# Grouped-query attention in a one-core backbone step: row maxima of two heads on the two halves of the contraction rows, and key tiles taken in twos

## The chip, the cores and the metric

The program runs on one core of one Trainium2 chip. The metric is the device time of one execution in microseconds (us); lower is better. Three executions of the kernel before gave 3754.33, 3758.16 and 3764.13 us (median 3758.16). A profile of a further execution was taken; that execution took 3772.03 us and its trace spans 3770.2 us.

## What is computed

The reference is one layer of a hybrid diffusion backbone on 256 context tokens and 2048 latent tokens: modulation, one joint input projection, three mixers in parallel (differential attention, grouped-query attention, a bidirectional state-space scan), an output projection with normalisation, and a SwiGLU feed-forward part. The change is in the grouped-query attention of the latent tokens (with one small part in the loading of the output projection's weights):

```
scale = 64 ** -0.5
qg = q.reshape(b, t, 2, 2, 64)           # 2 key/value heads, each with 2 query heads
s  = einsum('bqkgd,bskd->bkgqs', qg, k) * scale
p  = softmax(s, axis=-1)
o  = einsum('bkgqs,bskd->bqkgd', p, v)
```

There are 2048 queries and 2560 keys (2048 latent, 512 cached). Before the exponential, a bound near the row's maximum is subtracted.

## The kernel before

**Work and order.** `attention` (from L841) does the differential heads first, then the grouped heads. The order of instructions of TensorE, VectorE (DVE), ScalarE (ACT) and GpSimd (POOL) is the order in which the Python code emits them; generators are advanced by hand, each `yield` being a place where other work is put in. Each engine runs its own stream in order and waits on semaphores.

**Units.** The grouped heads are cut into 8 units (`units`, L934): a key/value head j and a block of 512 queries. A unit serves the two query heads r = 0, 1 of j. Queries and keys are held as two numbers each (a high part in F32R and a rest). `qa` is a tile [128, 2, 512] with the high parts in rows 0 to 63 and the rests in rows 64 to 127; `qb` has the high parts in rows 0 to 63 and, in row 64, the negated maxima. `gk[j][:, 0]` holds the keys' high parts twice (rows 0 to 63 and rows 64 to 127), `gk[j][0:64, 1]` the keys' rests, and row 64 of it ones.

**Maxima** (`maxima`, L945 to L969). For the unit after the one in hand: for each head r, each of 4 query tiles of 128 and each of 5 pieces of 512 keys, one matmul over 128 rows (tile `gm`, L959) into one PSUM bank, one DVE reduction over it (L960) and a `yield`: 40 steps. Then one reduction to `nm` (L962), and for each head four transposes of `nm` (L967) and a DVE copy into row 64 of `qb` (L968). The banks come from the ring `ps_t` of two. For unit 0, `wide=True`, done in the last steps of the differential heads: pieces of 1024 keys from the ring `ps_s` (two tiles of two banks), so three pieces (1024, 1024, 512) for a head and query tile.

**Weighted sum** (`weighted`, L971 to L1004). For each of 20 key tiles kt of 128 keys: four matmuls give the scores of both heads (L981 over 128 rows, L982 over 65 rows, into one two-bank tile of `ps_s`), and ACT takes the exponential of 1024 columns (L984) into a tile `ge` (ring of 5). After a `yield`, the values of key tile kt - 2 follow: one matmul for each head (L990), the two heads on the two halves of the output columns (64 each), and an addition of the exponentials into a running sum on DVE (kt % 5 in 1, 3) or POOL (L998, L1000). Then the second `yield`. So a unit has 44 yields.

**The driver** (L1333 to L1357). At each yield of `weighted` the maxima of the next unit are advanced by one step. At each second yield the tail of the unit before (`unit_tail`, L1006 to L1030: adding the two sums L1009, transposes L1013, sums over rows L1020), the context tokens' attention (`contexts`, in units 1 to 3; its lines here are L1068 to L1116) or, from unit 4 on, `OutProj.weights` (L1392) is advanced by one step. `OutProj.weights` loads a 512 KB piece of the output weights (L1396), yields, splits it into a high part on ACT (L1398) and a rest on DVE (L1399), and yields; its raw tiles have the tag `wor` in the pool `gsp` (two buffers).

**Loads.** `group_queries` (L936) is called at the beginning of a unit for the next one; SyncE's queue (SP) issues its two loads.

## Time and profile before

| | us |
|---|---|
| Three executions | 3754.33, 3758.16, 3764.13 |
| The profiled execution | 3772.03 |
| Its span in the trace | 3770.2 |
| TensorE (PE) busy | 3586.9 (95%) |
| DVE busy | 2490.2 (66%) |
| ACT busy, POOL busy | 1787.6 (47%), 1797.8 (48%) |
| Mean granted TensorE clock | 0.969 of full speed |
| The eight grouped units in the trace | from 1481.4 to 1956.8 |

In the rows, PE is TensorE's matmul stream and PEld its weight loads. Matmuls are pipelined: a record's own duration overlaps the next one's, so the cost of a matmul is the distance from its start to the next start. "idle before" is time in which the engine stood still before the instruction, with the instruction that ended it.

### The profile page before, as it was taken

To read this page: it belongs to the slowest core of one execution; us is meant where nothing else is said; L and a number is where in the kernel's file an instruction comes from. 1 tells how busy PE (TensorE), PEld (TensorE's weight loads), DVE (VectorE), ACT (ScalarE), POOL (GpSimd) and SP (SyncE) were. 2 spreads that over 40 slices of the span, in tenths; PEclk is the share of its full clock that TensorE was granted. 3 is DMA by queue.
4 is the path that set the end of the run, shared out by engine and by line. 5 is a ranking of instruction groups with operands and counts; after the bars stand their busy time and mean duration, and the time that the engine had idled before them with its cause. 6 is when DMAs were issued, how large, how long until landed. Compare 5 with 4: busy or idle time off the path is not lost.

```text
span 3770.2 us, 53905 instructions
## 1 busy us (share of the span) xinstructions
PE 3586.9 (95%) x20178; PEld 2884.0 (76%) x20178; DVE 2490.2 (66%) x4092; ACT 1787.6 (47%) x2890; POOL 1797.8 (48%) x1448
## 2 busy tenths in 40 slices
PE   6999899988999999999999989999999999999998
PEld 4888699984555555454458879999999999888886
DVE  3666766658889888767746776656556555465476
ACT  3555545546888885444334443334334333333232
POOL 3334356645788886445544567774233232011011
PEclk8999899998999999999999999999999999999999
DMA  5111244345311103001014656665454444645464
GB/s 199 49 46 46 76 126 124 119 130 164 97 34 42 36 22 83 14 26 48 23 62 165 209 190 216 213 216 182 153 186 164 160 154 163 231 160 175 153 217 156
DMA packets 265797, 473.65 MB, mean 126 GB/s; under 512 B 43480, under 2 KB 165752, under 8 KB 260928
## 3 DMA queue, kind: packets, MB, share of 16 engines
q1 hardware_dynamic: 247584, 456.72, 36.7%
q10 hardware_dynamic: 17232, 11.09, 1.1%
q8 instruction: 160, 2.62, 0.3%
q0 software_dynamic: 720, 2.38, 0.2%
q14 instruction: 101, 0.83, 0.1%
HBM read 345.72 MB, written 124.40 MB: 125 GB/s over the span
## 4 chain that ended last, share of the span: by engine, by line
PE 75%; DVE 9%; POOL 6%; issue 4%; DMA 3%; ACT 2%; SPq 0%; POOLq 0%; DVEq 0%; ACTq 0%
PE f L1685 6%; PE f L1684 6%; PE f L1683 6%; PE fy L1960 5%; PE fy L1962 5%; PE fy L1961 5%; PE ps L1174 4%; PE po L1234 4%; PE gpo L990 4%; PE px L225 3%; PE pt L1223 3%; PE gm L959 3%; PE gs L981 2%; PE gs L982 2%; PE opo L1447 2%
## 5 line engine op out<-in xcount | busy, mean ns | idle before, releaser
L1179 DVE TENSOR_SCALAR_CACHE_REDUCE e<-ps 128x1024 f32<-128x1024 f32 (+1 forms) x384 | 392.9, 1040 | 68.5 <-PE ps L1174 67.2
L1190 ACT ACTIVATE e<-e,nb 128x2560 f32<-128x2560 f32 x128 | 311.0, 2430 | 41.0 <-DVE nb L1184 40.9
L1960 PE MATMUL fy<-fp 128*128 128x512 f32 x792 | 308.7, 390 | 0.6 <-DVE fu L1823 0.6
L1962 PE MATMUL fy<-fp 128*128 128x512 f32 x792 | 308.7, 390 | 0.0
L1961 PE MATMUL fy<-fp 128*128 128x512 f32 x792 | 308.4, 389 | 0.0
L1212 POOL TENSOR_TENSOR e<-e,e 128x512 f32<-128x512 f32 x254 | 296.5, 1167 | 21.2
L1924 DVE TENSOR_TENSOR fp<-fo,fp 128x1536 fp32r<-128x1536 f32 (+1 forms) x110 | 208.7, 1911 | 140.5 <-ACT fp L1923 118.0
L960 DVE TENSOR_REDUCE gmx<-gm 128x1 f32<-128x512 f32 (+1 forms) x304 | 214.2, 715 | 120.0 <-PE gm L959 116.8
L1823 POOL TENSOR_TENSOR ft<-fu,fa 128x384 f32<-128x384 f32 x66 | 104.2, 1578 | 390.8 <-DVE fu L1823 342.8
L1991 POOL TENSOR_TENSOR fr<-fr,ln2b 128x1024 f32<-128x1024 f32 x17 | 54.0, 3178 | 490.6 <-DMA fo<-h_d 294.6
L1174 PE MATMUL ps<-dk,dq 96*128 96x512 f32 x640 | 244.9, 466 | 29.8 <-DVE e L1179 18.1
L1000 POOL TENSOR_TENSOR gag<-gag,ge 128x1024 f32<-128x1024 f32 x80 | 208.4, 2605 | 125.7 <-ACT ge L984 124.4
L984 ACT ACTIVATE ge<-gs 128x1024 f32<-128x1024 f32 x160 | 163.7, 1024 | 217.7 <-PE gs L982 215.3
L1923 ACT ACTIVATE fp<-fo 128x1536 fp32r<-128x1536 f32 (+1 forms) x110 | 157.2, 1442 | 195.1 <-PE fy L1962 163.8
L1211 POOL TENSOR_SCALAR e<-e,c 128x512 f32<-128x512 f32 x254 | 180.7, 711 | 115.2 <-DVE c L1203 104.9
L1174 PEld LDWEIGHTS ps<-dk,dq 96*128 96x128 f32 x640 | 101.0, 198 | 156.8 <-issue 72.1
L1224 ACT ACTIVATE wT<-pt 128x512 f32<-128x512 f32 x320 | 178.7, 591 | 67.8 <-PE pt L1223 67.1
L1234 PE MATMUL po<-wT,vl 128*64 128x256 f32 x1280 | 204.5, 407 | 0.0
L1223 PEld LDWEIGHTS pt<-cst,e 128*128 128x128 f32 x1280 | 160.7, 142 | 56.5 <-POOL e L1212 12.5
L1223 PE MATMUL pt<-cst,e 128*128 128x128 f32 x1280 | 197.1, 276 | 4.8 <-POOL e L1212 3.2
L225 PE MATMUL px<-xhTrue,wx 128*128 128x260 f32 (+2 forms) x864 | 182.1, 303 | 16.5 <-DVE l L374 7.0
L1685 PE MATMUL f<-fxt,wc 128*128 128x384 f32 x528 | 179.1, 339 | 2.6 <-DVE wc L1791 2.6
(454 smaller groups left out, 10613.0 us busy)
## 6 DMA issues: line engine op xcount, KB each, us to landing
fo<-in_wfo SPq DMA_DIRECT2D x110, 512.0 KB, 4.2
wq<-in_wfi SPq DMA_DIRECT2D x88, 512.0 KB, 3.7
wq<-ws_d SPq DMA_DIRECT2D x88, 512.0 KB, 4.2
h_d<-h SPq DMA_DIRECT2D x66, 384.0 KB, 3.0
wada<-in_w_ada SPq DMA_DIRECT2D x24, 1024.0 KB, 6.9
ws_d<-wq SPq DMA_DIRECT2D x44, 512.0 KB, 2.6
fo<-h_d SPq DMA_DIRECT2D x66, 256.0 KB, 4.1
fr<-x2T_d SPq DMA_DIRECT2D x20, 768.0 KB, 7.6
```

The lines of the kernel that those rows point to most:

```text
L225: PE.matmul(out, l, r, start=(i == 0), stop=(i == n - 1))
L1174: PE.matmul(ps[:, 512 * c:512 * c + 512], Q[0:96, m, qs], K[0:96, m, k0:k0 + 512], start=True, stop=True)
L1179: V.tensor_scalar(self.e[m][:, k0:k0 + w], ps[:, c:c + w], dscale, -3.4e38, ALU.mult, ALU.max, accum_out=mx[:, m, seen[m]:seen[m] + 1])
L1190: S.activation(self.e[m], self.e[m], AF.Exp, bias=self.nb[:, m:m + 1], accum_out=self.l[:, m:m + 1])
L1212: G.tensor_tensor(e0[:, a:b], e0[:, a:b], e1[:, a:b], ALU.add)
L1223: PE.transpose(pt[:, k], self.e[0][:, 128 * (4 * g + k):128 * (4 * g + k) + 128], ident)
L1234: PE.matmul(po[64 * e:64 * e + 64], hd.v[:, k + e], self.wT[:, k + e], start=(k == 0), stop=(k == NKT - 2))
L1683: PE.matmul(o, w[:, 0, c, cs], x[:, 0, k], start=(k == 0), stop=False)
L1685: PE.matmul(o, w[:, 1, c, cs], x[:, 0, k], start=False, stop=(k == 3))
L1960: PE.matmul(o, x[:, 0, ts_], x[:, 0, hs], start=(f == 0), stop=False)
L1961: PE.matmul(o, x[:, 0, ts_], x[:, 1, hs], start=False, stop=False)
L1962: PE.matmul(o, x[:, 1, ts_], x[:, 0, hs], start=False, stop=(f == NF - 1))
```

## The change

The queries' tile `qb` gets one more load: the high parts of head 1 into rows 64 to 127 of its first plane. `maxima` then takes two matmuls at a time, head 0 over rows 0 to 63 and head 1 over rows 64 to 127, each over 64 rows of `qb` and of the keys (the queries' rests no longer enter the maxima), into two banks: two tiles of `ps_t`, or the two halves of one tile of `ps_s` when wide. There are 20 steps of two matmuls; a narrow step has two reductions of 512 columns, a wide one a single reduction of 2 x 512. `weighted` takes two key tiles in an iteration (scores twice, yield, values twice, yield), so that it has 22 yields; the driver advances the tails, the contexts and the output weights at each yield instead of each second one. The ring `ge` has 6 buffers instead of 5. The raw output weights use the tag `osq` with one buffer, and four yields instead of one lie between load and split.

```
             load(qb[0:64], stk_d[8 + 2 * j:10 + 2 * j, 0:64, t0:t0 + 512].rearrange("r p t -> p r t"))
+            load(qb[64:128, 0], stk_d[9 + 2 * j, 0:64, t0:t0 + 512])
...
-            for r in range(2):
-                for q in range(4):
-                    ql = qa[:, r, 128 * q:128 * q + 128]
-                    pieces = range(0, KEYS, 1024 if wide else 512)
-                    for i, c in enumerate(pieces):
...
-                        for e in range(0, w, 512):
-                            PE.matmul(ps[:, e:e + 512], ql, gk[j][:, 0, c + e:c + e + 512], start=True, stop=True)
-                        V.tensor_reduce(mx[:, 4 * r + q, i:i + 1], ps[:, 0:w], AX.X, ALU.max)
-                        yield
+            for q in range(4):
+                for i in range(5):
+                    nm_ = f"gm{ui}_{q}{i}"
+                    if wide:
+                        p = ps_s.tile([128, 1024], F32, name=nm_, tag="s").rearrange("p (r t) -> p r t", r=2)
+                        ps = [p[:, r] for r in range(2)]
+                    else:
+                        ps = [ps_t.tile([128, 512], F32, name=f"{nm_}{r}", tag="t") for r in range(2)]
+                    for r in range(2):
+                        hs = slice(64 * r, 64 * r + 64)
+                        PE.matmul(ps[r], qb[hs, 0, 128 * q:128 * q + 128], gk[j][hs, 0, 512 * i:512 * i + 512],
+                                  start=True, stop=True)
+                    if wide:
+                        V.tensor_reduce(mx[:, q::4, i], p, AX.X, ALU.max)
+                    else:
+                        for r in range(2):
+                            V.tensor_reduce(mx[:, 4 * r + q, i:i + 1], ps[r], AX.X, ALU.max)
+                    yield
...
-            for kt in range(NKT + 2):
+            for kt in range(0, NKT + 2, 2):
                 if kt < NKT:
+                    scores(kt)
+                    scores(kt + 1)
                 yield
                 if kt >= 2:
+                    values(kt - 2)
+                    values(kt - 1)
                 yield
...
-            for i, _ in enumerate(weighted(ui, gsp, ps_o, tails)):
+            for _ in weighted(ui, gsp, ps_o, tails):
                 next(more, None)
-                if i % 2:
...
-            raw = pool.tile([128, 1024], F32, name=f"wor{k}", tag="wor")
+            raw = pool.tile([128, 1024], F32, name=f"wor{k}", tag="osq", bufs=1)
             nc.sync.dma_start(out=raw, in_=self.I["w_out"][128 * k:128 * k + 128, :])
-            yield
+            for _ in range(4):
+                yield
```

The new local functions `scores(kt)` and `values(k)` hold the same instructions as the loop's body before (L977 to L1000).

## Rows read from the trace of the kernel before

**Rows 1.** The page of the profiled execution: the busy times (part 1).

```profile
PE 3586.9 (95%) x20178; PEld 2884.0 (76%) x20178; DVE 2490.2 (66%) x4092; ACT 1787.6 (47%) x2890; POOL 1797.8 (48%) x1448
```

**Rows 2.** Busy time of each engine by stretch: first the wide maxima of unit 0, then units 0 to 7, a unit being counted from its first score matmul (stretch in us from the start of the span, its length, then busy us and instructions of PE, PEld, DVE, ACT and POOL, the granted clock, DMA share and GB/s).

```profile
1444.00:1481.40 37.40, 36.35 (x219) 20.34 (x217) 30.50 (x35) 14.83 (x24) 14.75 (x16) 1.00 0.27 60
1481.40:1535.60 54.20, 52.82 (x210) 25.65 (x209) 40.65 (x54) 21.09 (x23) 37.14 (x16) 1.00 0.40 110
1535.60:1612.30 76.70, 69.94 (x294) 36.68 (x292) 56.20 (x105) 34.34 (x66) 30.73 (x14) 0.93 0.05 14
1612.30:1678.90 66.60, 66.60 (x295) 35.00 (x293) 41.36 (x77) 30.73 (x52) 32.52 (x16) 1.00 0.07 22
1678.90:1736.10 57.20, 56.95 (x230) 28.16 (x228) 38.59 (x52) 21.68 (x22) 31.85 (x13) 0.97 0.07 22
1736.10:1798.70 62.60, 58.00 (x231) 28.24 (x229) 53.14 (x61) 29.14 (x30) 30.61 (x12) 0.97 0.21 68
1798.70:1854.90 56.20, 55.52 (x231) 27.82 (x229) 39.06 (x53) 21.69 (x22) 29.63 (x12) 1.00 0.07 19
1854.90:1910.90 56.00, 55.32 (x230) 27.77 (x228) 38.99 (x53) 21.68 (x22) 29.65 (x12) 1.00 0.02 5
1910.90:1956.80 45.90, 45.00 (x182) 19.88 (x180) 14.20 (x12) 21.59 (x22) 27.21 (x12) 1.00 0.09 29
```

**Rows 3.** PE in order of time in unit 4, one key tile in the steady part (start us, us, line, tiles, rows x columns; x4 at L990 is two matmuls of two passes each).

```profile
1780.35 1.08 PE L990 MATMUL gpo<-ge,vg 128*64 128x512 f32 x4
1781.35 0.50 PE L959 MATMUL gm<-gk,qa 128*128 128x512 f32 x1
1781.69 0.39 PE L981 MATMUL gs<-qa,gk 128*128 128x512 f32 x1
...
1782.38 0.40 PE L982 MATMUL gs<-qb,gk 65*128 65x512 f32 x1
1782.62 0.40 PE L959 MATMUL gm<-gk,qa 128*128 128x512 f32 x1
1782.94 1.08 PE L990 MATMUL gpo<-ge,vg 128*64 128x512 f32 x4
```

**Rows 4.** The same of unit 7, which has no maxima beside it: two starts of values one key tile apart, and the last three key tiles of values back to back.

```profile
1949.73 1.08 PE L990 MATMUL gpo<-ge,vg 128*64 128x512 f32 x4
...
1951.87 1.08 PE L990 MATMUL gpo<-ge,vg 128*64 128x512 f32 x4
...
1954.00 2.79 PE L990 MATMUL gpo<-ge,vg 128*64 128x512 f32 x12
```

**Rows 5.** PE in the context attention of unit 2: 256-column matmuls over 128 rows and over 64 rows in turn; one 128-row matmul lies between the two rows.

```profile
1630.92 0.38 PE L1071 MATMUL psc<-ckq,cqa 64*128 64x256 f32 x1
...
1631.54 0.38 PE L1071 MATMUL psc<-ckq,cqa 64*128 64x256 f32 x1
```

**Rows 6.** PE in the context attention of unit 1: four 256-column matmuls over 96 rows, and the next start.

```profile
1559.79 0.64 PE L1068 MATMUL psc<-ckq 96*128 96x256 f32 x4
1560.27 0.40 PE L981 MATMUL gs<-qa,gk 128*128 128x512 f32 x1
```

**Rows 7.** The groups of instructions from 1480 to 1960 us by line and shape (count | busy us, mean ns | idle us before and who ended it).

```profile
L960 DVE TENSOR_REDUCE gmx<-gm 128x1 f32<-128x512 f32 x280 | 189.7, 687 | 115.2 <-PE gm L959 112.2
...
L1000 DVE TENSOR_TENSOR gav<-gav,ge 128x1024 f32<-128x1024 f32 x48 | 72.8, 1516 | 22.2 <-ACT ge L984 22.2
...
L1399 DVE TENSOR_TENSOR wol<-wor,woh 128x1024 fp32r<-128x1024 f32 x8 | 14.6, 1824 | 0.0
...
L1074 DVE TENSOR_SCALAR_CACHE_REDUCE e0c<-psc 128x256 f32<-128x256 f32 x16 | 5.8, 421 | 2.7 <-PE psc L1071 2.7
```

**Rows 8.** DVE in order of time in unit 4, beside rows 3.

```profile
1783.05 0.69 DVE L960 TENSOR_REDUCE gmx<-gm 128x1 f32<-128x512 f32 x1 [0.40 <-PE gm L959]
1783.66 1.24 DVE L1000 TENSOR_TENSOR gav<-gav,ge 128x1024 f32<-128x1024 f32 x1
```

**Rows 9.** DVE in unit 4, a reduction that a maximum waits for.

```profile
1758.48 0.68 DVE L960 TENSOR_REDUCE gmx<-gm 128x1 f32<-128x512 f32 x1
```

**Rows 10.** PE in unit 4, the maximum that waits for it, behind a split of the output weights.

```profile
1759.21 0.51 PE L959 MATMUL gm<-gk,qa 128*128 128x512 f32 x1 [0.88 <-DVE gmx L960]
```

**Rows 11.** DVE in order of time at the end of unit 6.

```profile
1909.19 2.15 DVE L1000 TENSOR_TENSOR gav<-gav,ge 128x1024 f32<-128x1024 f32 x1
1911.38 1.29 DVE L968 CAST qb<-gpt 1x512 fp32r<-1x512 f32 x2
```

**Rows 12.** PE at the change from unit 5 to unit 6.

```profile
1851.73 0.51 PE L959 MATMUL gm<-gk,qa 128*128 128x512 f32 x1
...
1856.05 0.51 PE L982 MATMUL gs<-qb,gk 65*128 65x512 f32 x1 [0.68 <-DVE qb L968]
...
1866.45 0.48 PE L981 MATMUL gs<-qa,gk 128*128 128x512 f32 x1
```

**Rows 13.** PE in the wide maxima of unit 0: two starts of such maxima, four transposes (L1223) and two matmuls of values (L1234) apart.

```profile
1448.90 0.73 PE L959 MATMUL gm<-gk,qa 128*128 128x512 f32 x2
...
1450.58 0.73 PE L959 MATMUL gm<-gk,qa 128*128 128x512 f32 x2
```

**Rows 14.** The loads of queries at L855 on SP (issue ns min/median/max, first and last start us).

```profile
L855 SPq DMA_DIRECT2D qb<-stk_d x8: 579/579/624, 1038.0 to 1850.8; - x8
```

**Rows 15.** DMA issues by line: the lower-rows part of the queries (count, KB each, median us from issue to landing).

```profile
qb<-stk_d SPq DMA_DIRECT2D x8, 256.0 KB, 4.5
```

More of the change, by code (lines that the diff above doesn't have):

```diff
@@ L975, in weighted, with scores @@
             acc, held, es = {}, {}, {}
-            for kt in range(NKT + 2):
-                if kt < NKT:
-                    ks = slice(128 * kt, 128 * kt + 128)
-                    ps = ps_s.tile([128, 1024], F32, name=f"gs{ui}_{kt}", tag="s").rearrange("p (r t) -> p r t", r=2)
-                    for r in range(2):
-                        PE.matmul(ps[:, r], gk[j][:, 0, ks], qa[:, r], start=True, stop=False)
-                        PE.matmul(ps[:, r], gk[j][0:65, 1, ks], qb[0:65, r], start=False, stop=True)
-                    e = es[kt] = sp.tile([128, 2, 512], F32, name=f"ge{ui}_{kt}", tag="ge", bufs=5)
-                    S.activation(e, ps, AF.Exp, scale=gscale)
+            def scores(kt):
+                ks = slice(128 * kt, 128 * kt + 128)
+                ps = ps_s.tile([128, 1024], F32, name=f"gs{ui}_{kt}", tag="s").rearrange("p (r t) -> p r t", r=2)
+                for r in range(2):
+                    PE.matmul(ps[:, r], gk[j][:, 0, ks], qa[:, r], start=True, stop=False)
+                    PE.matmul(ps[:, r], gk[j][0:65, 1, ks], qb[0:65, r], start=False, stop=True)
+                e = es[kt] = sp.tile([128, 2, 512], F32, name=f"ge{ui}_{kt}", tag="ge", bufs=6)
+                S.activation(e, ps, AF.Exp, scale=gscale)
@@ new lines, in values @@
+            def values(k):
+                e = es.pop(k)
+                for r in range(2):
+                    PE.matmul(po[64 * r:64 * r + 64, :], gv[j][:, k], e[:, r], start=(k == 0), stop=(k == NKT - 1))
+                eng, nm = (V, "v") if k % 5 in (1, 3) else (G, "g")
+                if nm not in acc:
+                    if nm not in held:
+                        held[nm] = e
+                    else:
+                        acc[nm] = sp.tile([128, 2, 512], F32, name=f"ga{nm}{ui}", tag=f"ga{nm}")
+                        eng.tensor_tensor(acc[nm], held[nm], e, ALU.add)
+                else:
+                    eng.tensor_tensor(acc[nm], acc[nm], e, ALU.add)
@@ L985, in weighted @@
+            for kt in range(0, NKT + 2, 2):
+                if kt < NKT:
+                    scores(kt)
+                    scores(kt + 1)
                 yield
                 if kt >= 2:
-                    k = kt - 2
-                    e = es.pop(k)
-                    for r in range(2):
-                        PE.matmul(po[64 * r:64 * r + 64, :], gv[j][:, k], e[:, r],
-                                  start=(k == 0), stop=(k == NKT - 1))
-                    eng, nm = (V, "v") if k % 5 in (1, 3) else (G, "g")
```

27 lines of the change are left out of this document (8 added, 19 removed).

## The prediction

> **What bounds the kernel now.** Four views, from coarse to fine. The page's busy times come first: TensorE is busy for 95% of the span, the next engine for 66% [rows 1]. So the change counts by what it does to TensorE's stream. Next is the table by stretch, one for each unit [rows 2]. Units 5 and 6, with nothing but their own work, take 56.2 and 56.0 us, PE busy for 55.5 and 55.3 and DVE for 39: PE bounds them. Units 1 and 2 (context attention) take 76.7 and 66.6, unit 4 (output weights) 62.6; in units 1 and 4 PE stands still for 4 to 7 us. Unit 7, without maxima, takes 45.9. Then PE in order of time [rows 3]: a key tile takes 2.60 us (values to values), and each start follows as soon as the one before lets it. Last, DVE beside it [rows 7 to 11], for what a faster PE will ask of it. The stretch at stake is 37.4 us of wide maxima and 475 us of units.
>
> **Part 1, the steady key tile.** In rows 3 four score matmuls and two maxima belong to a key tile, and a start follows a start by 0.23 us while the array's use does not change. Values are two matmuls on the two halves of the columns, of two passes each: four records of over 0.5 us in 1.08 us, so two run at a time; the last twelve in a row take 2.79 us [rows 4], about 0.43 for a pair of passes. Streams alone are 6 x 0.233 + 2 x 0.43 = 2.26 us of the 2.60; the other 0.34 are two changes between full array and split columns, 0.17 each.
>
> A maximum over 64 rows brings in a third use of the array. The nearest rows are the context scores [rows 5]: going between 128 and 64 rows at each 256-column matmul costs (1631.54 - 1630.92) / 2 = 0.31 us, against 0.12 without such changes [rows 6]: 0.19 each. I take 0.18 for every change. The Trainium skill (TensorEngine Tiling (Array Packing), Key Properties) says that a change of tiling mode drains the engine, without a figure. The rows agree, and it speaks against this change, which brings a mode of its own into each step of maxima; without drains, by streams alone, the gain below would be 1.14 us and not 0.42.
>
> No row shows two matmuls on two halves of the rows. The bounds are two at a time, as with columns in rows 4 (0.23 us for the pair), and one after the other (0.47). I take the first: the same kind of split, on two banks.
>
> Two key tiles after the change: eight scores 1.87, two pairs 0.47, values 4 x 0.43 = 1.72, and four changes (full, rows, columns, rows, full) 0.72: 4.78 us. Before: 5.20. The gain is 0.42. Bounds: 0.80 if a change between two split modes costs nothing (4.40), 0.22 if the second half's weights load in the open (0.1 us a pair, as the 0.50 against 0.40 us of the two maxima in rows 3; 4.98), and a loss of 0.05 without concurrency (5.25).
>
> **Part 2, what DVE takes back.** DVE's work stays: 40 reductions of 687 ns a unit and 8 additions of 1516 ns on average [rows 7]; for two key tiles 2.75 + 1.21 = 3.96 us of 4.78. What shrinks is the slack. A reduction starts 0.43 us after its matmul [rows 3, 8] and takes 0.69, and PE follows 0.05 after its end [rows 9, 10]: a bank is free 1.2 us after its matmul's start. Before, two steps (2.60 us) lay between two uses of a bank: 1.4 us of slack. After, a pair fills both banks; the second reduction ends some 1.85 us after the pair's start, and the next pair comes after 2.3 (behind values) or 2.5 (behind scores): slack 0.4 to 0.6. An addition of 1.24 [rows 8] fits in; one of 2.15 [rows 11] holds the next pair up by 0.4 us. I take 0.1 us for two key tiles; bounds 0 and 0.4.
>
> Steady gain: eight iterations x (0.42 - 0.1) = 2.6 us a unit.
>
> **Part 3, ends of a unit.** From the last maximum to the next unit's first L982, which waits for the copies, is 4.32 us now (1851.73 to 1856.05) [rows 12]. DVE does the last addition and then two copies there [rows 11], in the same order after the change, while both last values now come before the transposes of `nm`, and the last of 23 steps falls behind the 22 yields: 3.9 to 4.9 us. I take a loss of 0.2. At the beginning no values lie between the first two pairs: scores of two key tiles, a pair, and then the second pair waits for the first's reductions. From L982 to the fifth key tile's scores is 10.4 us now [rows 12]; worked through with the steps above (first pair at 1.97, the halves of the second at 3.2 and 3.8, the third at 6.2, the fourth at 9.0, then the sums over rows) I get 11.3: a loss of 0.9, bounds 0.3 and 1.6.
>
> So a clean unit (0, 3, 5, 6) gains 2.6 - 1.1 = 1.5 us.
>
> **Part 4, the other stretches.** *Unit 7*: no pairs; two key tiles take 2 x 2.13 = 4.27 us now [rows 4], after that 1.87 + 1.72 + 0.35 = 3.94. Nine times 0.33: gain 3.0. *Wide maxima*: 24 tiles become 20; a slot goes from maxima through full-array transposes to values and back in 1.68 us [rows 13]. Each pair saves a stream (0.23) and adds a change (0.19): gain 0.8; DVE's reductions there keep their columns. *Output weights*: eight splits of 1.82 us on DVE [rows 7] spread over units 4 and 5 instead of 4 alone. They cost 4.6 us now: 62.6 - 56.1 of rows 2, less 1.9 for the granted clock of 0.97 there. Such a split makes a maximum wait 0.88 us [rows 10]; with less slack I take 1.0 each, 8 us: a loss of 3.4, bounds 0 and 6. The load has four yields for its way, so ACT meets it late enough; with one buffer SP waits for the split, and behind it stand only the loads and stores of a unit's end. *Contexts*: DVE's blocks there (four reads of 0.42 us [rows 7] and the like) are the same work met with less slack, while units 1 and 2 keep waits that a shorter PE stream can't use: I take 0, bounds a gain of 3 and a loss of 10. *Loads*: the new one is issued behind that of 1850.8 (0.58 us), which lands in 4.5 us [rows 14, 15], so by about 1856.5; the first pair that reads it starts at 1856.05 + 1.97 = 1858.0: hidden, with 1.5 us to spare, and a lateness beyond that would hold PE at each unit's first pair. The sixth `ge` buffer costs no time: it holds what the second key tile in hand needs.
>
> **Sum.** Clean units 4 x 1.5, unit 7 3.0, wide 0.8, output weights -3.4, contexts 0: a gain of 6.4 us. The profiled execution's 3772.0 us becomes 3765.6. It lay 13.9 us (0.4%) above the median of the runs; I take the same step from the median: 3758.2 - 6.4 = 3752 us. A measurement of this kernel tells about 0.3% (11.3 us) from no change: this is none.
>
> **Rivals.**
> A, *cheap changes, faster*: going between split rows and split columns costs nothing beyond the streams (4.40 us), with DVE's 3.96 still below. Eight iterations x 0.38 us x six units is 18 us more, and a part of the loss at the beginnings, 3 us, comes back: 3731. For it: both ends of those changes are split modes, which no row shows side by side; against it: rows 5 show a full price for rows.
> B, *DVE's lateness decides, slower*: with both banks filled together, every DVE job between two pairs that outlasts the slack of 0.4 to 0.6 us holds PE up. Price: eight blocks of context work at 1.0 us, 8 us, and 0.4 instead of 0.1 us in each of the 56 iterations with maxima, 17 us: 3777. It decides once additions take over 1.6 us, and their mean is 1.52 [rows 7]; against it: PE's waits in units 5 and 6 are below 1 us now [rows 2]. The Trainium skill (TensorEngine Tiling (Array Packing), PSUM Bottleneck) warns of this: tiling speeds up TensorE but not the emptying of PSUM, which may become the bound.
> C, *the pairs do not run together, slower*: 0.233 us more for each of 160 pairs, 37 us, less 6 us of waits that a longer stream hides: 3783. For it: no row shows the split; against it: the column split of rows 4 runs two at a time. Then the change doesn't do what it says.
>
> **How the numbers follow.** Forecast 50%, A 21%, B 18%, C 11%. The forecast's own range, from the bounds of parts 1 to 4, is 3737 to 3767. With A and B in it and C's end just outside the range is 3729 to 3781. Faster by over 0.3% (below 3747) is A and a fifth of the forecast: 0.32. Slower by over 0.3% (above 3769.5) is C and most of B: 0.26. The same: 0.42.
>
> **What would show it.** Right: the two `gm` matmuls of a pair overlapping, and the next start 0.3 to 0.45 us on; values of two key tiles in 1.9 us; 4.7 to 5.0 us between equal places of two iterations in unit 6; unit 7 at 43 us; about 1 us without work ahead of a unit's second pair. Wrong: the pairs' starts 0.23 us apart (C); PE waiting for `gmx` before most pairs (B); iterations of 4.4 us (A). A move of more than 10 us in units 1 and 2 would say that I have the contexts wrong, and a change outside 1444 to 1957 us that something else moved.

## The result: slower by 1.4%, and the profile after

The changed kernel takes 3815.1 us (median of four runs, 3804.2 to 3820.3) where the kernel before took 3761.1 in the same comparison: a ratio of 1.0139, 95% interval 1.0109 to 1.0170. The forecast was 3752 us; 3815 lies outside its range (3729 to 3781). The profiled execution has a span of 3812.4 us, 42.2 more than that of before. One execution of the kernel called e5 below (3983 us) fell into a slower state of the chip; the ratios and clocks given here leave it out.

The page's busy times say next to nothing: PE is busy for 6.5 us more than in [rows 1] in a kernel that gives it less work.

```profile
PE 3593.4 (94%) x20178; PEld 2876.3 (75%) x20178; DVE 2497.5 (66%) x4088; ACT 1780.8 (47%) x2890; POOL 1799.3 (47%) x1448
```

The table by stretch says where to look. It is cut as [rows 2] is: the wide maxima, then units 0 to 7 (stretch, length, busy us and count of PE, PEld, DVE, ACT and POOL, then the granted clock of TensorE, DMA share, GB/s).

```profile
1437.40:1473.10 35.70, 32.73 (x219) 17.30 (x217) 29.57 (x31) 14.87 (x24) 13.25 (x16) 1.00 0.29 67
1473.10:1527.80 54.70, 51.04 (x211) 24.38 (x210) 43.47 (x54) 20.68 (x24) 38.23 (x16) 1.00 0.39 102
1527.80:1616.40 88.60, 75.41 (x296) 37.88 (x293) 55.67 (x104) 33.63 (x66) 31.14 (x14) 0.83 0.05 14
1616.40:1693.20 76.80, 70.06 (x296) 35.01 (x293) 44.01 (x79) 30.07 (x53) 30.87 (x16) 0.91 0.07 19
1693.20:1755.40 62.20, 58.90 (x231) 28.32 (x229) 41.12 (x52) 21.13 (x23) 30.99 (x13) 0.89 0.08 24
1755.40:1826.40 71.00, 61.69 (x232) 28.77 (x229) 49.17 (x57) 24.59 (x26) 30.69 (x12) 0.88 0.13 39
1826.40:1892.50 66.10, 61.60 (x231) 30.33 (x229) 45.44 (x57) 24.77 (x26) 28.89 (x12) 0.85 0.16 50
1892.50:1955.50 63.00, 59.01 (x233) 28.15 (x230) 41.73 (x53) 20.95 (x22) 28.86 (x12) 0.89 0.02 5
1955.50:2001.10 45.60, 44.70 (x183) 23.57 (x180) 16.66 (x12) 20.28 (x21) 30.20 (x12) 0.93 0.05 16
```

Read three columns: length, PE busy, clock. Units 1 to 6 are 5 to 12 us longer than in [rows 2], and the granted clock, 0.93 to 1.00 there, is 0.83 to 0.91 now. At a granted clock of 0.5 (1.2 GHz instead of 2.4) a matmul of 512 columns starts 0.42 us after the one before it (the starts at 1899.20 and 1899.62 below), not 0.23, so a stretch in which PE's matmuls set the time loses its length times (1 - granted clock). With PE's idle time (length less busy) the whole stretch can be split in three:

| from the first maximum to the end of unit 7 | before | after | difference |
|---|---|---|---|
| length, us | 512.7 | 563.7 | +51.0 |
| PE idle | 16.3 | 48.5 | +32.2 |
| lost at 1.2 GHz (from the trace's unrounded clock) | 8.5 | 58.0 | +49.5 |
| the rest: PE's work at full clock | 487.9 | 457.2 | -30.7 |

(While PE stands still at 1.2 GHz half of the time counts in both shares, so the work is put too low: by 1.6 us here, by up to 6.8 in the experiments below.) So the change did save PE's work, by some 31 us. It bought 32 us of waits with it, and 50 us of half clock. Of the 32, 13 lie in units 1 and 2, beside the contexts.

The split is that of one execution. Outside this stretch, where the kernels' code is almost the same, the profiled executions lost between 78 us (e9 below) and 108 us (before) to the clock, so a few us in "lost" tell nothing. Each execution's mean clock is on record, though. By it (time times (1 - clock), averaged) the whole kernel lost 102 to 106 us before and 152 us after, 47 us more; that is the size of the table's 49.5.

PE's work in the steady part is as forecast. PE in order of time, in two key tiles of unit 6 (start us, us, line, tiles, rows x columns):

```profile
1936.31 0.50 PE L963 MATMUL gm<-gk,qb 64*128 64x512 f32 x2
1936.74 0.49 PE L990 MATMUL gs<-qa,gk 128*128 128x512 f32 x1
1937.08 0.40 PE L991 MATMUL gs<-qb,gk 65*128 65x512 f32 x1
...
1938.80 0.82 PE L963 MATMUL gm<-gk,qb 64*128 64x512 f32 x2
1939.56 1.94 PE L998 MATMUL gpo<-ge,vg 128*64 128x512 f32 x8
```

"x2" in 0.50 us: the two halves of a pair run together, and the next start is 0.43 us on; the values of two key tiles take 1.9. The second pair takes 0.82 us, as its second half starts 0.3 us late: it waits for its bank, behind an addition of 2.12 us on DVE. Such a wait counts as PE's work above. These two key tiles take 5.11 us, those without it 4.79 to 4.81.

The unit's end is not. The same view at the change from unit 5 to 6, which answers to [rows 12] (in brackets the idle time ahead, and what ended it):

```profile
1888.07 0.50 PE L963 MATMUL gm<-gk,qb 64*128 64x512 f32 x2
1888.50 1.94 PE L998 MATMUL gpo<-ge,vg 128*64 128x512 f32 x8
1892.03 0.68 PE L976 MATMUL gpt<-identr,nm 128*66 128x128 f32 x8 [1.59 <-DVE nm L971]
1892.54 0.45 PE L990 MATMUL gs<-qa,gk 128*128 128x512 f32 x1
1893.87 0.51 PE L991 MATMUL gs<-qb,gk 65*128 65x512 f32 x1 [0.89 <-DVE qb L977]
...
1897.13 1.10 PE L963 MATMUL gm<-gk,qb 64*128 64x512 f32 x2 [0.78 <-DVE gmx L969]
...
1898.97 0.42 PE L991 MATMUL gs<-qb,gk 65*128 65x512 f32 x1
1899.20 0.61 PE L990 MATMUL gs<-qa,gk 128*128 128x512 f32 x1
1899.62 0.63 PE L991 MATMUL gs<-qb,gk 65*128 65x512 f32 x1
...
1902.80 3.53 PE L998 MATMUL gpo<-ge,vg 128*64 128x512 f32 x8
```

Three waits, 3.3 us within 7; then, at 1899.2, with nothing left to wait for, the clock falls and the score matmuls go from 0.40 to 0.63 us and the values of two key tiles from 1.94 to 3.53. DVE beside it tells where the first wait comes from:

```profile
1886.31 1.29 DVE L969 TENSOR_REDUCE gmx<-gm 128x1 f32<-128x512 f32 x2
1887.51 3.03 DVE L1007 TENSOR_TENSOR gav<-gav,ge 128x1024 f32<-128x1024 f32 x1
1890.46 1.27 DVE L969 TENSOR_REDUCE gmx<-gm 128x1 f32<-128x512 f32 x2
1891.77 0.20 DVE L971 TENSOR_REDUCE nm<-gmx 128x8 fp32r<-128x40 f32 x1
1891.89 1.21 DVE L1007 TENSOR_TENSOR gav<-gav,ge 128x1024 f32<-128x1024 f32 x1
1893.13 1.29 DVE L977 CAST qb<-gpt 1x512 fp32r<-1x512 f32 x2
```

And GpSimd at that time:

```profile
1887.10 2.36 POOL L1007 TENSOR_TENSOR gag<-gag,ge 128x1024 f32<-128x1024 f32 x1 [2.44 <-ACT ge L993]
```

The addition that takes 3.03 us began 0.4 us after GpSimd's and ended 1.1 us after it; its twin at 1891.89, beside no GpSimd work, took 1.21. By that difference the last pair's two reductions are late, then `nm`, then the transposes. The times fit a DVE that stands still and is not slow: 1.21 us counted from GpSimd's end at 1889.46 gives 1890.67, against 1890.54. The Trainium skill (SBUF — State Buffer, Who interferes with whom) has the rule: a DVE instruction with two inputs in SBUF and a GpSimd instruction that reads SBUF share a read interface, and the later one is blocked until the other is through. These rows agree. It shows in the mean of the additions of the stretch (line, operation, shapes, count | busy us, mean ns | idle ahead):

```profile
L969 DVE TENSOR_REDUCE gmx<-gm 128x1 f32<-128x512 f32 x280 | 180.0, 683 | 152.5 <-PE gm L963 152.0
L1007 DVE TENSOR_TENSOR gav<-gav,ge 128x1024 f32<-128x1024 f32 x48 | 98.0, 2042 | 17.6 <-ACT ge L993 17.6
```

In [rows 7] they took 1516 ns. The reductions, from PSUM, keep their 0.69 us. It isn't the twos alone that bring the additions together: e1 below, with one key tile at a time, has 2016 ns, and e2, e4 and e6, without pairs, 1.99 to 2.16 us. The order of the kernel before happened to keep most of them apart.

### The profile page after: what moved, and what is told of

Same layout as the page of the kernel before. It is cut to its first block, busy times and chain, and to the rows that moved or that the text cites. A ratio compares the mean times of both kernels' runs of the same rounds, so it can differ in the third digit from the quotient of the medians.

```text
span 3812.4 us, 53913 instructions
## 1 busy us (share of the span) xinstructions
PE 3593.4 (94%) x20178; PEld 2876.3 (75%) x20178; DVE 2497.5 (66%) x4088; ACT 1780.8 (47%) x2890; POOL 1799.3 (47%) x1448
## 4 chain that ended last, share of the span: by engine, by line
PE 73%; DVE 11%; POOL 6%; issue 4%; DMA 3%; ACT 3%; SPq 0%; POOLq 0%; DVEq 0%; ACTq 0%
PE f L1701 6%; PE f L1700 6%; PE f L1699 6%; PE fy L1976 5%; PE fy L1978 5%; PE fy L1977 5%; PE ps L1190 4%; PE po L1250 4%; PE gpo L998 3%; PE px L225 3%; PE pt L1239 3%; PE gs L990 2%; PE gs L991 2%; PE gm L963 2%; PE opo L1463 1%
## 5 line engine op out<-in xcount | busy, mean ns | idle before, releaser
L969 DVE TENSOR_REDUCE gmx<-gm 128x1 f32<-128x512 f32 x280 | 180.0, 683 | 152.5 <-PE gm L963 152.0
L1239 PEld LDWEIGHTS pt<-cst,e 128*128 128x128 f32 x1280 | 157.7, 141 | 59.7 <-POOL e L1228 14.6
```

Source lines behind the costliest of these rows:

```text
L1239: PE.transpose(pt[:, k], self.e[0][:, 128 * (4 * g + k):128 * (4 * g + k) + 128], ident)
```

## The experiments

Each was run beside the kernel before. "Idle", "lost" and "work" are the three shares above, over the same stretch of the one profiled execution; the times are medians of all runs. In the cuts of code, "..." stands for lines left out.

| kernel | us | ratio to before, interval | idle | lost | work |
|---|---|---|---|---|---|
| before | 3761 to 3767 | 1 | 16 | 8.5 | 488 |
| after | 3815.1 | 1.0139 [1.0109, 1.0170] | 48 | 58 | 457 |
| e1 pairs only | 3785.1 | 1.0058 [1.0036, 1.0079] | 28 | 29 | 480 |
| e2 two key tiles only | 3798.7 | 1.0092 [1.0077, 1.0108] | 52 | 27 | 469 |
| e3 after, waits filled | 3795.5 | 1.0084 [1.0069, 1.0100] | 34 | 37 | 481 |
| e4 two tiles, maxima spread | 3761.6 | 0.9993 [0.9983, 1.0002] | 37 | 20 | 458 |
| e5 after, late additions out | 3773.2 | 1.0014 [1.0002, 1.0026] | 27 | 48 | 454 |
| e6 e4, late additions on GpSimd | 3756.2 | 0.9980 [0.9970, 0.9990] | 30 | 17 | 457 |
| e7 before, DVE hold | 3791.9 | 1.0071 [1.0055, 1.0087] | 30 | 29 | 483 |
| e8 before, hold filled | 3781.3 | 1.0044 [1.0027, 1.0061] | 17 | 10 | 503 |
| e9 before, hold filled, half rows | 3779.1 | 1.0041 [1.0027, 1.0056] | 21 | 14 | 503 |
| e10 e6 with pairs | 3777.2 | 1.0034 [1.0019, 1.0049] | 25 | 24 | 485 |
| e11 e6, weights on GpSimd | 3763.0 | 0.9996 [0.9985, 1.0008] | 37 | 24 | 452 |
| e12 after, early end | 3811.6 | 1.0115 [1.0094, 1.0136] | 47 | 58 | 463 |
| e13 e12, late additions on GpSimd | 3805.2 | 1.0109 [1.0094, 1.0124] | 40 | 51 | 463 |
| e14 e5 and e3 together | 3764.0 | 0.9996 [0.9982, 1.0010] | 17 | 22 | 475 |
| e15 e6, weights in quarters | 3775.3 | 1.0026 [1.0013, 1.0039] | 45 | 29 | 453 |

### Which half of the change costs it: e1, e2

e1 is the kernel before with the row pairs, one behind each key tile's scores; e2 the changed kernel with the old maxima, two at each yield.

```diff
 e1 (to before; maxima() as in after)
+load(qb[64:128, 0], stk_d[9 + 2 * j, 0:64, t0:t0 + 512])
-next(more, None)
-if i % 2:
+if i % 2 == 0:
+    next(more, None)
+else:
...
 e2 (to after; maxima() as in before, without the load to qb[64:128])
 next(more, None)
+next(more, None)
```

> The kernel before with the row pairs alone: maxima as changed, one step behind each key tile's scores, the loop still one key tile at a time, output weights as before. Theory T (the change's loss of some 50 us is TensorE's granted clock at 1.2 GHz, which falls after PE's waits at the ends of units and among the contexts, and those waits come from taking two key tiles and two banks at a time): per key tile 4 x 0.233 + 0.233 + 0.86 + 3 changes x 0.18 = 2.57 us against 2.60, waits between those of before and of the changed kernel, so 3750 to 3785 us, mean clock of the grouped stretch 0.94 to 0.98. Rival R (the row pairs themselves lower the clock or cost more than sized): 3795 or more, with 2.75 us or more per key tile in units 5 and 6. Rival W (the clock is a side show, PE's waits for DVE cost the time by themselves): time over that of before equals the growth of PE's waits, whatever the clock does.

> The changed kernel with the maxima of before (full array, high parts and rests, 40 steps), two steps at each yield; two key tiles at a time, six ge buffers and the output weights' new order stay. Steady: 8 x 0.233 + 4 x 0.233 + 1.72 + 0.35 = 4.87 us for two key tiles. Theory T: both banks are again filled together, so the waits at the ends of units and among the contexts stay, the clock of the grouped stretch stays at 0.88 to 0.94 and the time is within 15 us of the changed kernel (3800 to 3830). Rival R (it is the row pairs): the time of before or less, 3740 to 3765, clock 0.97 or more.

Both are slower than before, and both took work off PE, 8 and 19 us, and gave it back in idle time and clock. Neither half is the culprit alone. e1 stands at the upper end of its theory (3750 to 3785 us), e2 just below its own (3800 to 3830), with a clock of 0.95 in the stretch where 0.88 to 0.94 was expected. e2's steady two key tiles took 4.85 to 4.87 us.

### Does standing still bring the clock down: e3, e7, e8, e9

e3 puts 13 useless matmuls a unit into the three waits of the changed kernel. e7 makes a wait in the kernel before; e8 fills that wait, and e9 fills it with matmuls on 64 rows.

```diff
 e7 (to before), ahead of the first copy to qb, units 1 to 7's maxima
+V.tensor_reduce(hold[:, 0:1], gk[...][:, 0, 0:2048], AX.X, ALU.max)
 V.tensor_copy(qb[64:65, r], ...)
 e8: behind the second copy
...
+for _ in range(9):
+    PE.matmul(t, gk[...][:, 0, 0:128], gk[...][:, 0, 0:512], ...)
 e9: the same with gk[...][0:64, ...]
 e3 (to after): 4 such ahead of a unit's second pair, 6 behind the last pair, 3 behind the copies
```

> The changed kernel with matmuls of no use put where PE waits at the ends of a unit, from unit 0 to 6: six 512-column ones behind a unit's last values (ahead of the transposes of nm, where PE stood still 1.6 us in unit 5), three ahead of the next unit's scores, four between its first and second pair of maxima; 13 x 0.23 = 3.0 us of extra PE work a unit, 21 us in all, nearly all in time in which PE stood still. Theory T: PE does not fall silent there, fewer stretches at 1.2 GHz follow, the clock of the grouped stretch rises from 0.90 to 0.93 or more and the time FALLS by 10 to 30 us below the changed kernel, although work was added. Rival W (waits cost by themselves): the clock does not matter, the time stays within 5 us of the changed kernel or rises by up to 20.

> The kernel before with a useless DVE reduction over 2048 columns (about 2.2 us) just ahead of the first copy of the stabilisers at the end of units 0 to 6: PE, which needs the copies for the next unit's scores, waits that much longer at seven places, and nothing else changes. The waits alone are 7 x 2.2 = 15 us. Theory (a longer wait of PE at a unit's end brings the granted clock down to its lower level for the next stretch, and that costs more than the wait): granted clock below 0.95 in several units after, time lost to the clock over 20 us instead of 8, kernel 3785 to 3805 us. Rival (the clock doesn't mind such waits; the changed kernel lost it by its other matmuls): the clock as before, 3774 to 3780 us.

> The same as the kernel before with the hold of 2.2 us, with nine useless matmuls of 512 columns (9 x 0.23 = 2.1 us) on PE in the place of each wait, so that PE loses the same time but not by standing still. Theory (it is the standing still that brings the clock down): the clock as before, within 5 us of 3763 + 15 = 3778 us, and below the kernel with the hold alone by 10 us or more, although it has more work. Rival (the clock doesn't mind): both the same within 4 us, or this one slower.

> The kernel before with the hold of 2.2 us and nine useless matmuls in its place, as in the run with the hold and fill (3781 us, 10.2 us lost to the clock), but the nine matmuls read only 64 of the 128 rows of the array, one at a time. Theory (matmuls on half of the rows keep the clock up less than full ones, which is why the changed kernel lost twice the time to the clock that the kernel with two key tiles and full-array maxima lost with the same idle time): the clock falls as with the hold alone, 20 to 30 us lost, 3788 to 3796 us. Rival (any matmul counts as much as another, only standing still counts): as with the full matmuls, about 10 us lost, 3777 to 3785 us.

This is the clearest pair of the study. PE of e7 at the start of unit 6:

```profile
1863.19 0.50 PE L986 MATMUL gs<-qa,gk 128*128 128x512 f32 x1
1866.57 0.80 PE L987 MATMUL gs<-qb,gk 65*128 65x512 f32 x1 [2.88 <-DVE qb L973]
1867.17 0.63 PE L986 MATMUL gs<-qa,gk 128*128 128x512 f32 x1
```

And of e8 at the same place, `fl` being the useless matmuls (seven of the nine are in this view):

```profile
1857.78 1.78 PE L953 MATMUL fl<-gk 128*128 128x512 f32 x7
1859.50 1.08 PE L1005 MATMUL gpo<-ge,vg 128*64 128x512 f32 x4
1860.51 0.50 PE L996 MATMUL gs<-qa,gk 128*128 128x512 f32 x1
1861.76 0.49 PE L997 MATMUL gs<-qb,gk 65*128 65x512 f32 x1 [0.75 <-DVE qb L981]
1862.09 0.39 PE L996 MATMUL gs<-qa,gk 128*128 128x512 f32 x1
```

In e7 the first matmul behind the wait is already at half clock; in e8, with the same hold on DVE, it is not. e7 lost 29 us to the clock and e8 10 (over all executions, by the clocks on record, the whole kernels lost 123 and 101 us), and e8, with 15 us of useless matmuls (7 x 9 x 0.23), is 10.5 us faster, each of its four executions below each of e7's: standing still costs more than the wait. e3 says it of the changed kernel itself: 21 us of useless matmuls (7 x 13 x 0.23) made it 20 us faster. Of the theory of e9, that matmuls on half of the rows keep the clock up less, nothing is left: 14 us lost, 3779.1 us, and 103 us over all executions.

### What makes the waits: e5, e12, e13, e14

```diff
 e5 (to after)
 eng, nm = (V, "v") if k % 5 in (1, 3) else (G, "g")
+if nm == "v" and ui < 7 and k not in (1, 3):
+    return
 e12 (to after)
 scores(kt)
+if kt in (6, 10, 14):
+    yield 0          # one more pair here
 scores(kt + 1)
 e13 = e12 with
-eng, nm = (V, "v") if k % 5 in (1, 3) else (G, "g")
+eng, nm = (V, "v") if k % 5 in (1, 3) and (k < 13 or ui == 7) else (G, "g")
 e14 = e5 with the matmuls of e3
```

> The changed kernel without DVE's additions from the fourth key tile on in units 0 to 6 (seven of the eight of a unit; the row sums lack those key tiles, and a small constant stands in for them). GpSimd's additions stay, so DVE meets no GpSimd addition with one of its own. Theory (DVE's additions, lengthened from 1.52 to 2.04 us beside GpSimd's, come between the reductions, PE waits for banks, and the granted clock falls with the waits): PE's idle time between the first maximum and the last unit's end falls from 48 to about 25 us and the time lost to the clock from 58 to about 25, together some 55 us: 3755 to 3770 us for the kernel. Rival (the clock falls because of the pairs on half rows themselves, or because two key tiles in a row change PE's load): only the waits go, 3790 to 3800 us. Rival (the waits at a unit's end come from the chain of sums, transposes and copies, not from additions): below 10 us of gain, over 3805 us.

> The changed kernel with three of its pairs issued earlier, one more between the scores of two key tiles in the iterations of key tiles 6, 10 and 14, so that the sums over rows and both transposes of a unit end lie ahead of the last two key tiles' values, and the copies run behind those values. The three pairs pay two changes of the array's use each, about 3 x 0.36 = 1.1 us a unit. Theory (the waits of 0.9 to 1.6 us at a unit's end are where the time goes: each costs itself and, by the lower clock in the next stretch, more): PE's idle time falls from 48 to about 30 us, the time lost to the clock from 58 to 25 to 30 us, kernel 3768 to 3785 us. Rival (additions lengthened by GpSimd make the waits wherever the maxima lie): idle over 40 us and over 3795 us. Rival (pairs keep the clock down by themselves): the clock loss stays over 45 us, over 3795 us.

> The same, with the additions of key tiles 13, 16 and 18 moved from DVE to GpSimd in units 0 to 6. Theory (both causes, the order at the unit's end and DVE's late additions): 8 to 20 us below the one with the order alone, 3753 to 3768 us. Rival (with the end mended the additions are covered): within 4 us of it. Against the version with full-array maxima (3756 us): the pairs' 0.07 us for two key tiles is too little to tell.

> The changed kernel both without DVE's late additions (as in the run at 3773 us, which leaves them out of the row sums) and with the 13 useless matmuls of 512 columns a unit in PE's waits at the change of units. The clean units 3, 5 and 6 had 1.1 us of idle time each without the additions and still lost 6.8, 6.8 and 1.7 us to the clock; with the matmuls alone they had 0.6 to 1.7 us and lost 3.4 to 5.1. Theory (even the three waits of 0.3 to 0.8 us around a unit's start bring the clock down): with all of them filled the three units lose no time to the clock; all units together 15 to 30 us instead of 47.8, and the kernel 3755 to 3772 us, no slower than without the matmuls though they take up to 13 x 0.23 x 7 = 21 us. Rival (the row pairs keep the clock down by themselves, also between waits): the clean units still lose 3 us or more each, and the kernel takes 3775 to 3790 us.

e5 leaves out six of the seven additions of a unit (its expectation says seven of eight). It is 42 us faster than the changed kernel, near the theory's 3755 to 3770: 22 of the 32 us of waits are gone. But only 10 of the 50 us of clock came back in the profiled execution, the longest of nine; over the nine, by the clocks on record, it was 18 of 47.

17 of e5's 27 us of waits are in units 1 and 2. The changed kernel has 20 there (7 before), so leaving the additions out takes away only 3. Its rows show two other sources. The context's transposes (L1114, L1131) take banks from the ring of the maxima, and wait 15 times for a reduction, 9.1 us in all; before, none did. And a pair waits 3.57 us behind the context's four combinations on DVE, with two inputs in SBUF, while GpSimd does three additions from 1553.59 to 1561.92:

```profile
1557.02 5.97 DVE L1105 SCALAR_TENSOR_TENSOR e0c<-e1c,cc,e0c 128x256 f32<-128x256 f32 x4
1563.65 1.10 PE L963 MATMUL gm<-gk,qb 64*128 64x512 f32 x2 [3.57 <-DVE gmx L969]
```

In the kernel before, the same four took 1.67 us. No run takes the contexts' part away.

In a unit without other work e5's waits are 0.1 to 0.8 us long (1.1 us in all), and the clock still falls. Units 3 and 5 of e5, by stretch:

```profile
1685.40:1744.50 59.10, 57.98 (x230) 27.87 (x229) 29.50 (x47) 20.91 (x23) 29.38 (x13) 0.88 0.08 25
1805.40:1865.10 59.70, 58.57 (x232) 28.77 (x230) 35.47 (x51) 24.52 (x26) 28.00 (x12) 0.89 0.17 55
```

The same two in e14, where these waits are filled:

```profile
1676.50:1732.50 56.00, 56.00 (x242) 28.50 (x241) 29.59 (x47) 20.91 (x22) 27.99 (x12) 0.97 0.08 22
1790.40:1848.30 57.90, 57.90 (x243) 29.27 (x242) 35.02 (x51) 24.61 (x26) 28.02 (x12) 0.94 0.16 52
```

No idle time of PE is on record in them, and the clock is 0.97 and 0.94 instead of 0.88 and 0.89: most of the loss was the waits', and a part (1.7 and 3.4 us a unit) was not. e14 lies between theory and rival there, and takes 3764.0 us, as the theory had it. What PE did before the clock fell is the same in each of units 3 to 6. This is unit 4 (`gpl`: the sums over rows of the unit before):

```profile
1742.21 1.95 PE L1053 MATMUL gpl<-cst,gav 128*128 128x2 f32 x16
1744.02 0.47 PE L1005 MATMUL gs<-qa,gk 128*128 128x512 f32 x1
...
1744.59 0.63 PE L1005 MATMUL gs<-qa,gk 128*128 128x512 f32 x1
```

These are 16 matmuls of only two columns, in which PE counts as busy. In each of the four units the clock fell once, 0.6 to 2.0 us after the last of them began. It is so in the changed kernel too: 17 of its 58 us were lost in six falls 0.4 to 1.6 us after the last of a unit's row sums began, with no wait of over 0.3 us in the 10 us ahead; the other 41 us, in ten falls, came after waits. No run moves the row sums, so that they bring the clock down is read from this order and not shown.

e12 missed its theory. The waits at its unit's end are gone, but an extra pair stands only one key tile's scores behind the pair ahead of it, and in unit 6 an addition of 3.00 us, begun 0.45 us after one of GpSimd's, made PE wait 1.45 us there: idle time 47 us, as without the edit. A wait was moved, not removed, and the clock stayed with it. e13 took 7 us off idle time and clock each in the profiled executions, but the medians differ by 6.3 us and the runs overlap: that lies between its rival (within 4 us of e12) and its theory (8 us and more), and decides for neither.

### Versions without the waits, and the pairs again: e4, e6, e10, e11, e15

e4 keeps two key tiles at a time and full-array maxima, but puts one behind each head's two score matmuls, and at a unit's end the reduction to `nm` ahead of the last two values and the transposes between them. e6 moves three late additions. e10 puts the pairs back in, one behind each key tile's scores. e11 and e15 change the output weights' subtraction in e6.

```diff
 e4 (to e2)
 for r in range(2):
     PE.matmul(ps[:, r], gk[j][:, 0, ks], qa[:, r], ...)
     PE.matmul(ps[:, r], gk[j][0:65, 1, ks], qb[0:65, r], ...)
+    yield 0          # one step of maxima
...
 values(kt - 2)
+if kt == NKT:
+    yield 0          # the transposes, two steps
+    yield 0
 values(kt - 1)
 e6 (to e4): e13's line for the additions
 e10 (to e6): maxima() as in after, one yield a key tile
 e11 (to e6)
-nc.vector.tensor_tensor(self.wl[:, k], raw, self.wh[:, k], ALU.subtract)
+nc.gpsimd.tensor_tensor(self.wl[:, k], raw, self.wh[:, k], ALU.subtract)
 e15 (to e6)
+for c in range(0, 1024, 256):
+    nc.vector.tensor_tensor(self.wl[:, k, c:c + 256], raw[:, c:c + 256], ...)
+    yield
```

> The kernel of e2_twos_only with the full-array maxima spread out: one step after each head's two score matmuls (four in an iteration, 0.70 us apart, against 0.64 to 0.69 us of a reduction), none behind the values; at the end of a unit the reduction to nm comes ahead of the last two values and the transposes between them, as before. Theory T: no two banks are filled back to back, PE waits little, the clock stays near that of before (0.96 to 0.98), two key tiles take 4.87 to 5.0 us, and the time is 3730 to 3755, below before. Rival W2 (DVE's 0.69 us behind 0.70 us of PE leaves no slack, so PE waits inside each iteration): 5.2 us or more for two key tiles and 3765 or more.

> The kernel with two key tiles at a time and full-array maxima spread one behind each head's scores (3761.6 us), with the additions of key tiles 13, 16 and 18 moved from DVE to GpSimd in units 0 to 6, so that DVE has no addition to do while the last maxima, the sums over rows and the copies of the stabilisers are due. Theory (DVE's late additions cause the waits at the ends of units and the lower clock that follows): 10 to 15 us less, 3747 to 3752 us. Rival (the copies' chain alone makes those waits): within 4 us of 3761.6. Rival (GpSimd, with 15 additions of 2.6 us in a unit of 54 us, becomes late for the exp buffers): slower than 3765 us.

> The kernel of 3756.2 us (two key tiles, full-array maxima behind each head's scores, no late additions on DVE; idle 30, clock 17 us) with the change's row pairs in the place of its maxima, a pair behind each key tile's scores. Theory (the pairs themselves are the second cause of the lower clock): about as much idle time (25 to 35 us), but 35 to 50 us lost to the clock: 3775 to 3790 us. Rival (only the waits and their placing count): clock 15 to 20 us, 3753 to 3762 us. Rival (the pairs' two streams at once are worth more than they cost once the waits are gone): below 3750 us.

> The kernel of 3756.2 us with the output weights' eight subtractions (1.8 to 2.0 us each) moved from DVE to GpSimd. Units 4 and 5 take 63.2 and 59.6 us there against 52.4 of units 3 and 6. Theory (these subtractions keep reductions from freeing banks, and PE's waits cost twice through the clock): units 4 and 5 together 8 to 14 us shorter, 3743 to 3749 us. Rival (GpSimd, with 15 additions of 2.6 us and four subtractions in a unit, frees the exp buffers too late): the same or slower, 3756 to 3765 us.

> The kernel of 3756.2 us (two key tiles, full-array maxima spread, late additions on GpSimd) with each subtraction of the output weights (1.8 to 2.0 us on DVE) done in four parts of 256 columns at four yields. Theory (a DVE job that outlasts the slack between two maxima makes PE wait, shorter ones fit in): units 4 and 5, 63.2 and 59.6 us there, lose 8 us together: 3746 to 3752 us. Rival (DVE's sum of work in these units decides, not the length of one job; four starts add to it): 3754 to 3760 us.

e6 is the one kernel that is faster than before, by 0.2% (interval 0.1 to 0.3%): the work of the changed kernel (457 us) with 30 us of idle time instead of 48 and 17 us of clock instead of 58. The move of the late additions gave 5.3 us against e4, less than the 10 to 15 expected. e4 says the same without the additions' move: the order of the maxima and transposes alone is worth 37 us against e2. At 3761.6 us it still missed its theory (3730 to 3755), for it waits 37 us, and stayed below its rival (3765).

e10 answers a question about the pairs. Units 3 and 6 of e10:

```profile
1689.30:1746.10 56.80, 56.51 (x231) 26.59 (x229) 35.26 (x50) 21.71 (x22) 39.62 (x17) 1.00 0.08 25
1873.30:1930.10 56.80, 56.49 (x231) 26.63 (x229) 35.01 (x50) 21.70 (x22) 36.16 (x16) 1.00 0.02 6
```

Pairs throughout, 0.3 us of idle time, full clock: pairs alone don't bring it down, and its 24 us of clock, against 35 to 50 expected, came from the units with other work. Its time fell where the theory had put it, for another reason: it is slower than e6 by its work, 27 us more. Two key tiles take 5.30 us against 4.87: a pair between two key tiles' scores has its changes of the array's use for itself, five changes where e6 has two, and the second pair takes 0.80 us in place of 0.50, its halves one behind the other.

e15 and e11 both missed their theories, and show the collision once more. e15 is slower than its rival had it, too. The subtraction in e6 (whole) and in e15 (a quarter of the columns), over units 4 and 5:

```profile
L1416 DVE TENSOR_TENSOR wol<-wor,woh 128x1024 fp32r<-128x1024 f32 x8 | 14.6, 1821 | 8.2 <-ACT woh L1415 8.2
```

```profile
L1417 DVE TENSOR_TENSOR wol<-wor,woh 128x256 fp32r<-128x256 f32 x20 | 22.7, 1157 | 5.3 <-ACT woh L1415 5.2
```

A quarter of the columns takes 0.64 of the time on average. Each start can meet a GpSimd addition; one that did, on DVE:

```profile
1758.33 0.43 DVE L1417 TENSOR_TENSOR wol<-wor,woh 128x256 fp32r<-128x256 f32 x1 [1.08 <-ACT woh L1415]
1758.68 3.41 DVE L1001 TENSOR_TENSOR gav<-gav,ge 128x1024 f32<-128x1024 f32 x1
1762.02 2.56 DVE L1417 TENSOR_TENSOR wol<-wor,woh 128x256 fp32r<-128x256 f32 x1
1764.50 1.28 DVE L960 TENSOR_REDUCE gmx<-gm 128x1 f32<-128x512 f32 x2
```

The same instruction, 0.43 and 2.56 us. GpSimd was in three additions from 1756.10 to 1764.30, and PE waited:

```profile
1765.23 0.79 PE L959 MATMUL gm<-gk,qa 128*128 128x512 f32 x1 [4.78 <-DVE gmx L960]
```

In e11 unit 4 shrank from 63.2 to 54.7 us, but units 5 and 6 grew from 59.6 and 52.3 to 65.4 and 64.4, with 9.4 and 8.8 us of idle time: the rival of GpSimd's lateness.

## Why the prediction was wrong, by its own steps

**The step that failed is the sum itself: it had no term for the granted clock.** It read the clock in rows 2 (0.93 to 1.00), took 1.9 us of unit 4 for it, and let it stand. The clock went to 0.83 to 0.91 in units 1 to 6 and cost 49.5 us, about the whole difference. With it left out, work and idle time give -30.7 + 32.2: no change, which is what was forecast, though as a small difference between two larger terms than mine; that they cancel is luck. e7 against e8 shows that waits cost clock beyond themselves. The waits failed in size with it: 13 of the 32 us lie in units 1 and 2, for which the sum took nothing.

*Part 1* was right. Two key tiles without a wait take 4.79 to 4.81 us (forecast 4.78), pairs run together, e2's 4.85 to 4.87 without pairs fits the price of a change, and unit 7's iterations take 3.94 (forecast 3.94). Rivals A (4.40) and C (pairs one after the other) are out.

*Part 2* failed in size. It priced DVE's waits at 0.1 us for two key tiles, with additions of 1.52 us. They took 2.04, since the new order brought them under GpSimd's, and six iterations of unit 6 (1918.88 to 1949.14) took 5.04 us on average, 0.26 over 4.78. The price of a single long addition was right: one of 2.15 us was to hold a pair up by 0.4, and one of 2.12 did by 0.3. (A unit has seven additions on DVE and not eight; [rows 7] show 48 of the 56.) Rival B named the condition, additions over 1.6 us, and the side. Its price, 3777, lacked the clock too. What spoke against it, that the mean was 1.52 in the kernel before, was an argument from an order that the change takes away. e5 shows this share: 22 us of waits. A longer addition need not cost that: e4 and e6 have them too (1.99 and 2.01 us), and wait for less, since their maxima stand apart.

*Part 3* was too small at a unit's end. From the last maximum to the first L991 it is 5.80 us (1888.07 to 1893.87), not 4.32 + 0.2. From there to the fifth key tile's scores it is 14.6 (to 1908.48), of which 3.4 went to half clock; the 11.2 that are left are the 11.3 forecast. The second pair's wait at the start, 0.78 us here, was foreseen; that half clock would follow three short waits within 7 us was not.

*Part 4*: the wide maxima gained 1.7 us (0.8 forecast). Unit 7 gained 0.3 and not 3.0; it began at half clock and lost 3.4 us to it (0.93). The sum leaves out unit 4's own steady gain, 1.5 us, and rival A's price counts six units where B's counts seven. Units 4 and 5 lost 18.3 us; what exceeds the clean units 3 and 6 (62.6 on average) there is 8.4 + 3.5 = 11.9, clock included, against the 8 forecast for the output weights. Units 1 and 2 lost 22 us where I took 0 with a bound of 10; the text said that a move of more than 10 us there would say that I had the contexts wrong, and I had: their transposes wait for the maxima's banks, and their DVE work met GpSimd's additions (5.97 us for 1.67). *Loads* and buffers cost nothing that these rows show.

**What stays open.** By the table, kernels with pairs lost 1.0 to 1.8 us of clock for each us of idle time (after, e1, e3, e5, e10, e12, e13, e14); those without lost 0.5 to 1.0 (before, e2, e4, e6 to e9, e11, e15). e2 and after, with nearly the same idle time, lost 27 and 58. Part of that stands behind the row sums: with pairs and two key tiles at a time (after, e3, e5, e12, e13, e14) the clock fell after 4 to 7 of the 7 row sums of the stretch, 12 to 19 us in all, in the other kernels after 1 to 4 of them, 2 to 7 us. Without these e2 and after still lost 24 and 41. Matmuls on half the rows filled a wait as well as full ones (e9), pairs almost without waits lost nothing (units 3 and 6 of e10), and the number of changes of the array's use doesn't explain it: e10 has five for two key tiles, the changed kernel four. Why the rest differs, where the waits lie or something else, no run tells.

The Trainium skill (TensorE: Matmul & The Clock Gate, A second HAM failure mode) describes a kernel whose PE idles briefly between groups of matmuls, cycling through PSUM banks, and whose clock goes back and forth between its two levels. The rows of unit 5 to 6 and e7 agree, with waits of 0.78 to 1.59 us and of 2.88. By it alone the forecast would have had a rival of this sign; units 3 to 7 lost 3.4 to 10.2 us each to the clock.

## What to carry to other kernels

Where one engine is busy for 95% of the time, a change that takes its work away has to be asked what fills the time: if it becomes short waits, the clock may fall behind them and cost more than the work saved. Put a term for the granted clock into the sum, priced from a stretch of the profile where it is low, as soon as the change makes new waits close together. And a mean duration is that of an order: additions on DVE that had mostly been clear of GpSimd's met them once the steps around them moved.

## What the runs showed of the hardware that was not expected

A DVE instruction of 256 columns with both inputs in SBUF took 0.43 us in one place and 2.56 in another, beside GpSimd additions of 2.7 us, and one of 1024 columns between them took 3.41: the short job was held for as long as the long one. In e14 the clock fell 0.6 to 2.0 us after the last of 16 matmuls of two columns began, in four units for which the trace shows no idle time of PE. Useless matmuls in PE's waits made a kernel 20 us faster (e3 against after). And two matmuls on the two halves of the rows, on two banks, ran together at the price of one: 0.50 us for both, next start after 0.43 with the change of the array's use.
